# A two-layer mixer and mixture-of-experts trunk: layer 0's normalised rows from POOL to VectorE, routing by counting pairs, and a later place for layer 1's residual products

## Chip, cores and metric

One core of one Trainium2 chip. The metric is the device time of one execution in microseconds (us). The engines are named as in the profile: PE is TensorE, DVE VectorE, ACT ScalarE, POOL GpSimd, and SP the engine whose queue issues most DMAs.

## What is computed

Two layers of a trunk over 256 context rows (`ctx`) and 256 latent rows (`x`), each row 1024 wide, all in float32. Each layer mixes the rows (attention, a recurrence, latent attention, one output projection), adds the result, and then runs a mixture of 16 experts of which every row uses two. What the change touches is the end of the mixer and the choice of the experts:

```python
xl = xl + mod_l[2] * yl
hl = modulate(rms_norm(xl, norm_ffn[layer]), mod_l[3], mod_l[4])      # the normalised rows
...
scores = jax.nn.sigmoid(jnp.matmul(t, router_w))                      # 16 experts in 4 groups of 4
sel = scores + router_bias
group_score = jnp.sum(lax.top_k(sel.reshape(-1, 4, 4), 2)[0], axis=-1)
...                                                                   # the best group, in it the best 2 experts
w = jnp.take_along_axis(scores, e_idx, axis=-1); w = w / jnp.sum(w, axis=-1, keepdims=True)
y = sum over the 2 chosen experts of w * down(silu(gate(t)) * up(t))
```

Layer 0 does this for all 512 rows, layer 1 for the 256 latent rows alone.

## The kernel before

Rows are held as tiles of 128; in layer 0 there are four, t = 0 and 1 context (s = 0), t = 2 and 3 latent (s = 1). Large products are split: a weight slice is copied to a high part `wh` on ACT (line 183), the low part `wl` is the difference, made on DVE (line 184), and three products per slice go to PE (lines 164 to 166). Four `wh` and four `wl` buffers let ACT and DVE run ahead of PE by four slices.

`after_mix` is the end of the mixer. For s = 0 and then s = 1 it multiplies by the output weights in two halves of columns (`proj(s, 0)`, `proj(s, 1)`: eight weight slices and 48 products each), and its `put` adds the gated result to the rows `x[t]` (lines 918 and 919, DVE) and squares them (line 922, ACT). `flip` turns the rows for the router (line 932, PE; copied at line 934, ACT). `route(s)` adds the squares, takes the reciprocal root `rr` (lines 942 and 173 on DVE, 174 on POOL), multiplies by the router's weights (line 947, PE), copies the result (line 950, DVE), turns it (line 953, PE), sums and scales it to logits (lines 955 and 958, DVE), and calls `norm(s)` and `choose`.

`norm(s)`, in layer 0 alone, makes the normalised rows h2 = x * r * A2 + B2, which the experts read: for t < 3 the product with r on ACT (line 969), the one with A2 on POOL (line 970), for t = 3 both on DVE (line 972), and always the addition of B2 on POOL (line 973). A2 and B2 are rows that POOL's DMA queue loads (line 351) when their buffers come free: those of s = 1 after the work on the tiles of s = 0. `keep` writes the rows to DRAM (line 982, for t = 2 and 3 line 1609), from where the experts gather them.

`choose` finds for two tiles at once the best group and two experts (lines 1043 to 1094). The sums of all six pairs of a group give the group's score (lines 1048 to 1051). Then `first_max` is called three times, for the group, the first and the second expert: a maximum, two comparisons with it, another maximum, and two instructions of `put` that mark it. What comes out is `asg` (line 1082: 1 where a row uses an expert), and the two weights. `ranks` counts on PE how many rows before this one chose the same expert (lines 1105 and 1106), line 1109 makes `rm` from it on DVE, and line 978 the one-hot matrix `oh`.

`pick_early` (line 1369, PE) gathers the rows of the first fixed expert with `oh`: t = 0 and 1 before, t = 2 and 3 behind the ranks of s = 1. Its result is copied at lines 1382 (ACT) and 1383 (DVE), and the products of that expert begin. `slots` meanwhile orders the other experts by their numbers of rows; `rperm` (line 1253) names them, and SP can load their weights only when it has read it (line 1632).

In layer 1 the same `after_mix` runs for s = 1 without `norm`, and `moe1` follows: `onehot` (line 1347) and `pick` (line 1358) gather the rows of the first pair of experts, line 1461 multiplies them. The rows themselves are put into four PSUM banks by products with the identity (line 1976: four products, which the profile counts as eight). Weights flow through 20 buffers of 1 MB; SP loads the next (line 1326) when PE has finished with the buffer.

The order on each engine is set by a scheduler, which takes instructions by its own estimate of when they can run; `in_order` and `issue_after` add edges to it.

Of the kernel before, what the change touches and what calls it, by code (L numbers as in the profile page):

```python
# [73 lines left out]
class Net:  # L74
# [802 lines left out]
    def after_mix(self, l, XP, tiles, mh, ml, x, h2, ws, oh=None):  # L877
# [5 lines left out]
        with self.pool("am", side="left" if l else "right") as T:  # L883
# [52 lines left out]
            def route(s):  # L936
# [6 lines left out]
                self.rstd(ss, 2, D, rt["r"][:, i0:i0 + 2])  # L943
                a = self.at()
# [7 lines left out]
                for i in range(2):  # L952
                    nc.tensor.transpose(tp[:, i * 128:(i + 1) * 128], lt[:, i * 128:(i + 1) * 128], self.ident)
# [6 lines left out]
                if l == 0:  # L960
                    norm(s)
                self.choose(T, rt, lg, i0)

            def norm(s):
                A2, B2 = G[s][3:]
                for t in (2 * s, 2 * s + 1):
                    h, r = h2[t], rt["r"][:, t:t + 1]
                    if t < 3:
                        nc.scalar.activation(h, x[t], AF.Copy, scale=r)
                        nc.gpsimd.tensor_tensor(h, h, A2, op=OP.mult)  # L970
                    else:
                        nc.vector.scalar_tensor_tensor(h, x[t], r, A2, op0=OP.mult, op1=OP.mult)
                    nc.gpsimd.tensor_tensor(h, h, B2, op=OP.add)
# [40 lines left out]
    def routing_tiles(self, pool, l, nt):  # L1014
        r = {}
        r["r"] = pool.tile([128, nt], F32, name="rr")
        for n, w, dt in (("oh1", NE, F32), ("oh2", NE, F32), ("rk", NE, F32), ("rm", NE, F32), ("asg", NE, BF),
                         ("w1", 1, F32), ("w2", 1, F32)):
# [8 lines left out]
        r["we"] = pool.tile([128, nt, NE], F32, name="rwe")  # L1027
# [6 lines left out]
    def choose(self, T, rt, lg, i0):  # L1034
# [3 lines left out]
        t2 = slice(i0, i0 + 2)  # L1038

# [4 lines left out]
        V.scalar_tensor_tensor(sel, th, 0.5, self.rb[:, None, :].to_broadcast([128, 2, NE]), op0=OP.mult, op1=OP.add)  # L1044
# [6 lines left out]
        V.tensor_reduce(m1.rearrange("p t g -> p (t g)"), ps, axis=AX.X, op=OP.max)  # L1051
        V.tensor_scalar(sc, th, 0.5, 0.5, op0=OP.mult, op1=OP.add)

        def first_max(src, n):

            mx = T.tile([128, 2], F32, name="cmx")
            fm = T.tile([128, 2], F32, name="cfm")
            cd = T.tile([128, 2, NE], F32, name="ccd")
            V.tensor_reduce(mx, src, axis=AX.X, op=OP.max)
            for i in range(2):  # L1060
                V.scalar_tensor_tensor(cd[:, i, :n], src[:, i], mx[:, i:i + 1], self.c("adj")[:, NE - n:], op0=OP.is_ge,
                                       op1=OP.mult)
            V.tensor_reduce(fm, cd[:, :, :n], axis=AX.X, op=OP.max)
            return cd, fm

        def put(dst, cd, fm, n, op, f):

            for i in range(2):
                V.tensor_scalar(dst[:, i], cd[:, i, :n], fm[:, i:i + 1], f, op0=op, op1=OP.mult)
        g = tl("g", 4)  # L1070
        cd, fm = first_max(m1, 4)
        put(g, cd, fm, 4, OP.is_lt, -BIG)
        V.tensor_add(s4, s4, g.rearrange("p t g -> p (t g)")[:, :, None].to_broadcast([128, 8, 4]))
        o1, o2 = rt["oh1"][:, t2], rt["oh2"][:, t2]
        pen = tl("pen", NE)
        cd, fm = first_max(sel, NE)
        put(pen, cd, fm, NE, OP.is_equal, -10.0 * BIG)
        V.tensor_add(sel, sel, pen)
        put(o1, cd, fm, NE, OP.is_equal, 1.0)
        cd, fm = first_max(sel, NE)  # L1080
        put(o2, cd, fm, NE, OP.is_equal, 1.0)
        V.tensor_add(rt["asg"][:, t2], o1, o2)
        pr, w1, w2, tot = tl("pr", NE), tl("w1", 1), tl("w2", 1), tl("tot", 1)
        V.tensor_mul(pr, o1, sc)
        V.tensor_reduce(w1, pr, axis=AX.X, op=OP.add)
        V.tensor_mul(pr, o2, sc)
        V.tensor_reduce(w2, pr, axis=AX.X, op=OP.add)
        V.tensor_add(tot, w1, w2)
        V.reciprocal(tot, tot)
        V.tensor_mul(rt["w1"][:, t2], w1, tot)  # L1090
        V.tensor_mul(rt["w2"][:, t2], w2, tot)
        if "idx" not in rt:
            V.tensor_mul(rt["we"], o1, rt["w1"].to_broadcast([128, 2, NE]))
            V.tensor_mul(pr, o2, rt["w2"].to_broadcast([128, 2, NE]))
            V.tensor_add(rt["we"], rt["we"], pr)

    def ranks(self, T, rt, i0):
# [12 lines left out]
        V.tensor_copy(rt["rk"][:, t2], p3)  # L1110
# [95 lines left out]
    def slots(self, T, P, rt):  # L1206
# [59 lines left out]
        V.tensor_mul(we, rt["oh1"], rt["w1"].to_broadcast([128, nt, NE]))  # L1266
        V.tensor_mul(pr, rt["oh2"], rt["w2"].to_broadcast([128, nt, NE]))
        V.tensor_add(we, we, pr)
# [41 lines left out]
        for i, o in enumerate((rt["oh1"], rt["oh2"])):  # L1310
# [548 lines left out]
    def moe1(self, rt, x):  # L1859
# [6 lines left out]
        with ExitStack() as st:  # L1866
# [90 lines left out]
            for p in range(NE // 2):  # L1957
# [366 lines left out]
```

## Time and profile before

| | us |
|---|---|
| median of 3 runs | 1535.23 (1534.76 to 1537.57) |
| profiled execution, its own time | 1536.22 |
| its span, first to last instruction | 1534.4 |
| PE busy | 1423.4 (93%) |
| DVE busy | 928.3 (61%) |
| ACT busy | 672.4 (44%) |
| POOL busy | 110.2 (7%) |
| mean granted clock of PE | 0.977 |

How to read it: the span lacks 1.8 us of the execution's own time, which lie around it. Each engine works through its own queue in order, and waits where an operand is late. A row's idle time stands in brackets behind it, with what ended it. Two stretches matter here, the end of layer 0's mixer (about 575 to 660 us) and that of layer 1 (about 1285 to 1310 us). Behind each of them lies a long stretch of experts.

### The profile page before, as it was taken

What the parts mean: (1) busy time and instruction counts of PE and PEld (TensorE: products, weight loads), DVE (VectorE), ACT (ScalarE), POOL (GpSimd) and SP (SyncE); (2) the same over time, 40 slices, a digit from 0 to 9 for tenths busy, and PEclk for the clock granted to TensorE, in tenths of its full rate; (3) what the DMA queues carried; (4) which work ended last, traced back from release to release, by engine and by line L of the source; (5) the groups of instructions that cost most, each with busy time, mean ns of one, the idle gap of its engine ahead of it and who ended that gap; (6) DMA issues with size and microseconds to landing.
All of it is one profiled execution on the core that took longest, in us unless ns stands there. A gap on an engine that the chain in (4) does not pass through costs nothing. (4 is left out here: it accounts for less than half of the span.)

```text
span 1534.4 us, 20655 instructions
## 1 busy us (share of the span) xinstructions
PE 1423.4 (93%) x7431; PEld 931.3 (61%) x7431; DVE 928.3 (61%) x2149; ACT 672.4 (44%) x1343; POOL 110.2 (7%) x126
## 2 busy tenths in 40 slices
PE   5989999999999998789999986899999997999996
PEld 3756675587675666665545645688788775333332
DVE  4575556967554268898544748757977786423322
ACT  3343345735443235274544625555775553211112
POOL 1110000010000003200000021300001000000000
PEclk9999999999999999799999998999999999999999
DMA  7536335331125885599999994432333268999994
GB/s 314 213 138 229 138 110 199 134 112 57 56 86 204 321 304 129 196 329 366 421 420 422 420 369 164 179 110 87 121 128 100 96 226 347 362 422 424 424 423 180
DMA packets 56921, 363.63 MB, mean 237 GB/s; under 512 B 6384, under 2 KB 6384, under 8 KB 18672
## 3 DMA queue, kind: packets, MB, share of 16 engines
q1 hardware_dynamic: 47376, 328.49, 54.7%
q0 software_dynamic: 6544, 23.60, 4.7%
q10 hardware_dynamic: 2896, 10.19, 1.7%
q8 instruction: 60, 0.98, 0.3%
q14 instruction: 45, 0.37, 0.1%
HBM read 350.72 MB, written 11.54 MB: 236 GB/s over the span
## 5 line engine op out<-in xcount | busy, mean ns | idle before, releaser
L184 DVE TENSOR_TENSOR wl<-w,wh 128x512 fp32r<-128x512 f32 (+2 forms) x456 | 309.7, 696 | 183.4 <-ACT wh L183 167.2
L183 ACT CAST wh<-w 128x512 fp32r<-128x512 f32 (+2 forms) x456 | 271.0, 607 | 252.6 <-PE acc L244 126.3
L243 PE MATMUL acc<-hh,wh 128*128 128x512 f32 (+1 forms) x528 | 183.9, 348 | 0.2 <-ACT wh L183 0.2
L245 PE MATMUL acc<-hh,wl 128*128 128x512 f32 (+1 forms) x528 | 179.9, 341 | 1.4 <-DVE wl L184 1.4
L244 PE MATMUL acc<-hl,wh 128*128 128x512 f32 (+1 forms) x528 | 180.5, 342 | 0.0
L1461 PE MATMUL at<-w,xT 128*64 128x512 f32 x512 | 122.0, 600 | 1.1 <-DVE act L1466 0.8
L243 PEld LDWEIGHTS acc<-hh,wh 128*128 128x128 f32 x528 | 100.2, 190 | 31.3 <-issue 10.8
L245 PEld LDWEIGHTS acc<-hh,wl 128*128 128x128 f32 x528 | 100.3, 190 | 14.2 <-DVE wl L184 2.7
L244 PEld LDWEIGHTS acc<-hl,wh 128*128 128x128 f32 x528 | 100.2, 190 | 12.0 <-issue 2.1
L165 PE MATMUL acc<-wl,hh 128*128 128x512 f32 (+3 forms) x256 | 90.8, 355 | 8.9 <-DVE wl L184 5.4
L164 PE MATMUL acc<-wh,hh 128*128 128x512 f32 (+3 forms) x256 | 89.4, 352 | 8.5 <-ACT wh L183 3.1
L166 PE MATMUL acc<-wh,hl 128*128 128x512 f32 (+3 forms) x256 | 88.7, 349 | 0.0
L526 ACT ACTIVATE p<-at,nm 128x512 f32<-128x512 f32 (+1 forms) x96 | 59.1, 618 | 45.6 <-DVE nm L525 45.1
L1461 PE MATMUL acc<-w,xT 128*64 128x512 f32 x320 | 75.7, 599 | 1.5 <-DMA w<-in_moeu_dram 1.5
L174 POOL TENSOR_TENSOR rr<-rv,mhalf 128x1 f32<-128x1 f32 (+2 forms) x41 | 34.4, 841 | 544.0 <-DVE rv L173 538.4
L1461 PEld LDWEIGHTS at<-w,xT 128*64 128x64 f32 x512 | 33.5, 136 | 59.4 <-issue 54.9
L525 DVE TENSOR_REDUCE nm<-at 128x1 f32<-128x512 f32 (+1 forms) x96 | 56.5, 595 | 12.5 <-PE at L640 7.7
L243 PE MATMUL acc<-oh,wh 128*128 128x512 f32 (+1 forms) x160 | 59.5, 373 | 0.0
L165 PEld LDWEIGHTS acc<-wl,hh 128*128 128x128 f32 x256 | 49.1, 192 | 16.1 <-DVE wl L184 11.9
L164 PEld LDWEIGHTS acc<-wh,hh 128*128 128x128 f32 x256 | 48.8, 191 | 15.5 <-issue 4.8
L1484 PE MATMUL at<-w,aT 128*64 128x512 f32 x256 | 56.7, 595 | 0.0
L244 PE MATMUL acc<-ol,wh 128*128 128x512 f32 (+1 forms) x160 | 55.9, 350 | 0.0
(512 smaller groups left out, 2647.0 us busy)
## 6 DMA issues: line engine op xcount, KB each, us to landing
w<-in_moeg_dram SPq DMA_DIRECT2D x64, 1024.0 KB, 18.1
w<-in_moeu_dram SPq DMA_DIRECT2D x64, 1024.0 KB, 13.3
w<-in_moed_dram SPq DMA_DIRECT2D x64, 1024.0 KB, 16.8
w<-in_wmod_dram SPq DMA_DIRECT2D x48, 1024.0 KB, 6.1
w<-in_wg_dram SPq DMA_DIRECT2D x24, 1024.0 KB, 4.8
w<-in_wb_dram SPq DMA_DIRECT2D x12, 1024.0 KB, 5.0
w<-in_wout_dram SPq DMA_DIRECT2D x8, 1024.0 KB, 7.3
w<-in_wx_dram SPq DMA_DIRECT2D x4, 1024.0 KB, 8.8
```

Source lines behind the costliest of these rows:

```text
L164: nc.tensor.matmul(acc, ah, bh, start=start, stop=False)
L165: nc.tensor.matmul(acc, ah, bl, start=False, stop=False)
L166: nc.tensor.matmul(acc, al, bh, start=False, stop=stop)
L183: nc.scalar.copy(h, src)
L184: self.cut = nc.vector.tensor_sub(l, src, h.bitcast(F32))
L243: nc.tensor.matmul(a[:, :n], h[:, i, :], hh[:, k, t0:], start=k == 0, stop=False)
L244: nc.tensor.matmul(a[:, :n], h[:, i, :], hl[:, k, t0:], start=False, stop=False)
L245: nc.tensor.matmul(a[:, :n], l[:, i, :], hh[:, k, t0:], start=False, stop=k == kc - 1)
L525: nc.vector.tensor_reduce(nm, sc[h][:, :nk], axis=AX.X, op=OP.max, negate=True)
L526: nc.scalar.activation(p[:, :nk], sc[h][:, :nk], AF.Exp, bias=nm, accum_out=sm)
L1461: nc.tensor.matmul(a[i * 64:i * 64 + 64], xT[:, k], ws[i][k // 4][:, k % 4], start=k == 0, stop=k == 7, tile_position=(0, i * 64))
L1484: self.nc.tensor.matmul(ya[n][64 * j:64 * j + 64], aT[:, k, 64 * j:64 * j + 64], w[k // 2][:, k % 2, n * 512:(n + 1) * 512], start=k == 0, ...
```

## The change

In layer 0, A2 now multiplies each half of the columns as soon as `put` has it (DVE), and `norm(t)` is one DVE instruction that multiplies by r and adds B2. It is called for t = 2s right after `rr`, and for t = 2s + 1 inside `choose`, behind the call of the tanh. ACT and POOL do nothing for the rows any more. `choose` compares each expert with the three others of its group: one that wins at least two comparisons is among the two best, and a group that wins all three is chosen. One reduction adds the wins. The two experts are kept apart no longer, `we` holds both weights; layer 0 finds the first and second late in `slots`. The copy `rk` (line 1110) is gone. In layer 1 the four residual products come behind the transposition of the logits.

```diff
@@ after_mix, put
                     nc.vector.tensor_add(x[t][:, cols], x[t][:, cols], y)
+                    if l == 0:
+                        nc.vector.tensor_mul(h2[t][:, cols], x[t][:, cols], G[s][3][:, cols])
@@ after_mix, route
                 self.rstd(ss, 2, D, rt["r"][:, i0:i0 + 2])
+                if l == 0:
+                    norm(2 * s)
...
-                    nc.tensor.transpose(tp[:, i * 128:(i + 1) * 128], lt[:, i * 128:(i + 1) * 128], self.ident)
+                    self.routed = nc.tensor.transpose(tp[:, i * 128:(i + 1) * 128], lt[:, i * 128:(i + 1) * 128], self.ident)
...
-                if l == 0:
-                    norm(s)
-                self.choose(T, rt, lg, i0)
-
-            def norm(s):
-                A2, B2 = G[s][3:]
-                for t in (2 * s, 2 * s + 1):
-                    h, r = h2[t], rt["r"][:, t:t + 1]
-                    if t < 3:
-                        nc.scalar.activation(h, x[t], AF.Copy, scale=r)
-                        nc.gpsimd.tensor_tensor(h, h, A2, op=OP.mult)
-                    else:
-                        nc.vector.scalar_tensor_tensor(h, x[t], r, A2, op0=OP.mult, op1=OP.mult)
-                    nc.gpsimd.tensor_tensor(h, h, B2, op=OP.add)
+                self.choose(T, rt, lg, i0, functools.partial(norm, 2 * s + 1) if l == 0 else None)
+
+            def norm(t):
+                nc.vector.scalar_tensor_tensor(h2[t], h2[t], rt["r"][:, t:t + 1], G[t // 2][4], op0=OP.mult, op1=OP.add)
@@ choose
         nc.scalar.activation(th, lg, AF.Tanh, scale=0.5)
+        if mid:
+            mid()
...
+        def wins(src, n, name):
+            c = T.tile([128, n, 4, 3], F32, name="cc" + name)
+            w = T.tile([128, n, 4], F32, name="cw" + name)
+            for d in (1, 2, 3):
+                V.tensor_tensor(c[:, :, :4 - d, d - 1], src[:, :, :4 - d], src[:, :, d:], op=OP.is_ge)
+                V.tensor_tensor(c[:, :, d:, 3 - d], src[:, :, d:], src[:, :, :4 - d], op=OP.is_gt)
+            V.tensor_reduce(w, c, axis=AX.X, op=OP.add)
+            return w
+        we = wins(s4, 8, "e")
+        wg = wins(m1, 2, "g").rearrange("p t g -> p (t g)")
+        V.tensor_scalar(wg, wg, 2.5, None, op0=OP.is_ge)
+        asg = rt["asg"][:, t2]
+        V.scalar_tensor_tensor(asg.rearrange("p t (g e) -> p (t g) e", g=4), we, 1.5, wg[:, :, None].to_broadcast([128, 8, 4]),
+                               op0=OP.is_ge, op1=OP.mult)
         V.tensor_scalar(sc, th, 0.5, 0.5, op0=OP.mult, op1=OP.add)
-        def first_max(src, n):
...
+        pr, tot = tl("pr", NE), tl("tot", 1)
+        V.tensor_mul(pr, sc, asg)
+        V.tensor_reduce(tot, pr, axis=AX.X, op=OP.add)
         V.reciprocal(tot, tot)
...
+        V.tensor_mul(rt["we"][:, t2], pr, tot.to_broadcast(fe))
@@ slots, its last part; three instructions that made we are gone from its middle
+        V.tensor_tensor(cd, rt["asg"], self.c("adj")[:, None, :].to_broadcast(fe), op=OP.mult)
+        V.tensor_reduce(fm, cd, axis=AX.X, op=OP.max)
+        V.tensor_tensor(o1, cd, fm[:, :, None].to_broadcast(fe), op=OP.is_equal)
+        V.tensor_sub(o2, rt["asg"], o1)
+        for i, o in enumerate((o1, o2)):
...
+            V.tensor_mul(cd, rt["we"], o)
+            V.tensor_reduce(rt[f"w{i + 1}"].rearrange("p t o -> p (t o)"), cd, axis=AX.X, op=OP.add)
@@ moe1
-                    for t, xt in enumerate(x):
-                        for n in range(2):
-                            nc.tensor.matmul(res[t][n], self.ident, xt[:, n * 512:(n + 1) * 512], start=True, stop=False)
+                    with self.tc.issue_after(self.routed.ins):
...
```

On POOL, in layer 0 from the loads of s = 1 to the first gather, the queue was this (h_5002 to h_5005 are h2 of t = 0 to 3, A_5255, B_5256 and g_5251 rows of s = 1):

```order
L351 DMA g_5251<-modd_91 128x2x512
L174 TENSOR_TENSOR rr<-rv,mhalf 128x2
L970 TENSOR_TENSOR h_5002<-h_5002,A_5031 128x1024
L973 TENSOR_TENSOR h_5002<-h_5002,B_5032 128x1024
L970 TENSOR_TENSOR h_5003<-h_5003,A_5031 128x1024
L982 DMA h2d<-h_5002 128x1024
L351 DMA A_5255<-modd_92 128x2x512
L973 TENSOR_TENSOR h_5003<-h_5003,B_5032 128x1024
L351 DMA B_5256<-modd_91 128x2x512
L982 DMA h2d<-h_5003 128x1024
L174 TENSOR_TENSOR rr<-rv,mhalf 128x2
L970 TENSOR_TENSOR h_5004<-h_5004,A_5255 128x1024
```

and is now this (A_5256 and B_5257 are the rows of s = 1):

```order
L351 DMA g_5252<-modd_91 128x2x512
L351 DMA A_5256<-modd_92 128x2x512
L174 TENSOR_TENSOR rr<-rv,mhalf 128x2
L976 DMA h2d<-h_5002 128x1024
L351 DMA B_5257<-modd_91 128x2x512
L976 DMA h2d<-h_5003 128x1024
L174 TENSOR_TENSOR rr<-rv,mhalf 128x2
L1588 DMA h2d<-h_5004 128x1024
L1588 DMA h2d<-h_5005 128x1024
```

All six multiplications and additions are gone, and the load of A2 for s = 1 stands ahead of `rr`.

On DVE, in layer 0's `route(1)`, from the root's operand to the tanh's result, the rows were these:

```order
L173 TENSOR_SCALAR rv<-ss_5573 128x2
L950 COPY ytmp<-at 128x256
L972 SCALAR_TENSOR_TENSOR h_5005<-x_4998,rr,A_5255 128x1024
L955 TENSOR_REDUCE lg<-tp 128x32
L958 SCALAR_TENSOR_TENSOR lg<-lg,rr,cl 128x16 x2
L1044 SCALAR_TENSOR_TENSOR csel<-cth,rb 128x32
```

and now they are these:

```order
L173 TENSOR_SCALAR rv<-ss_5553 128x2
L184 TENSOR_TENSOR wl<-w,wh 128x512
L967 SCALAR_TENSOR_TENSOR h_5004<-h_5004,rr,B_5257 128x1024
L954 COPY ytmp<-at 128x256
L967 SCALAR_TENSOR_TENSOR h_5005<-h_5005,rr,B_5257 128x1024
L959 TENSOR_REDUCE lg<-tp 128x32
L962 SCALAR_TENSOR_TENSOR lg<-lg,rr,cl 128x16 x2
L1040 SCALAR_TENSOR_TENSOR csel<-cth,rb 128x32
```

One normalisation stands ahead of the copy of the router's products, and the other ahead of the logits' reduction.

On PE, at the end of layer 1's mixer, the residual products (L1976, into acc) stood among the router's:

```order
L947 MATMUL at<-xT,wr 32x256 x4
L1976 MATMUL acc<-x_12289,cp 128x512
L932 MATMUL tp<-cp,x_12289 128x128 x4
L1976 MATMUL acc<-x_12289,cp 128x512
L932 MATMUL tp<-cp,x_12290 128x128 x4
L1976 MATMUL acc<-x_12290,cp 128x512
L947 MATMUL at<-xT,wr 32x256 x4
L1976 MATMUL acc<-x_12290,cp 128x512
L953 MATMUL tp<-cp,ytmp 128x128 x2
L1106 LDWEIGHTS trib
```

and now stand together:

```order
L951 MATMUL at<-xT,wr 32x256 x4
L934 MATMUL tp<-cp,x_12254 128x128 x4
L934 MATMUL tp<-cp,x_12255 128x128 x4
L951 MATMUL at<-xT,wr 32x256 x4
L957 MATMUL tp<-cp,ytmp 128x128 x2
L1956 MATMUL acc<-x_12254,cp 128x512 x2
L1956 MATMUL acc<-x_12255,cp 128x512 x2
L1080 LDWEIGHTS trib
```

All four are between the transposition of the logits and the first product of the ranks.

## Rows read from the trace of the kernel before

**Rows 1.** Stretches in layer 0: PE, PEld, DVE, ACT, POOL busy us, clock, DMA share, GB/s.

```profile
575.00:585.00 10.00, 10.00 (x49) 8.19 (x48) 6.75 (x11) 6.20 (x13) 0.00 (x0) 1.00 0.50 95
...
610.30:617.30 7.00, 4.95 (x18) 3.78 (x17) 5.05 (x14) 3.67 (x9) 0.00 (x0) 0.51 0.87 286
...
645.00:650.00 5.00, 4.93 (x26) 4.90 (x27) 3.39 (x14) 0.00 (x0) 2.06 (x3) 0.50 0.01 1
```

**Rows 2.** Timeline of PE, 601 to 652 us: start, length, row, [idle before <-releaser].

```profile
602.74 0.50 PE L165 MATMUL acc<-wl,hh 128*128 128x512 f32 x1 [1.06 <-DVE wl L184]
...
609.21 0.50 PE L165 MATMUL acc<-wl,hh 128*128 128x512 f32 x1 [2.02 <-DVE wl L184]
...
613.66 0.66 PE L953 MATMUL tp<-cp,ytmp 128*128 128x128 f32 x2 [2.05 <-DVE ytmp L950]
...
630.85 0.69 PE L953 MATMUL tp<-cp,ytmp 128*128 128x128 f32 x2 [0.55 <-DVE ytmp L950]
631.33 5.13 PE L1369 MATMUL tp<-oh,h 128*128 128x128 f32 x32
...
643.96 0.17 PE L1106 MATMUL at<-rasg,trib 128*128 128x16 bf16 x1 [7.46 <-DVE rasg L1082]
...
651.77 0.48 PE L164 MATMUL acc<-wh,xh 128*128 128x512 f32 x1
```

**Rows 3.** Timeline of POOL, 596 to 639 us.

```profile
596.91 2.42 POOL L970 TENSOR_TENSOR h<-h,A 128x1024 f32<-128x1024 f32 x1 [1.26 <-ACT h L969]
...
634.17 4.64 POOL L973 TENSOR_TENSOR h<-h,B 128x1024 f32<-128x1024 f32 x2
```

**Rows 4.** Timeline of DVE, 595 to 644 us.

```profile
595.68 0.69 DVE L184 TENSOR_TENSOR wl<-w,wh 128x512 fp32r<-128x512 f32 x1 [0.84 <-ACT wh L183]
597.37 12.39 DVE L184 TENSOR_TENSOR wl<-w,wh 128x512 fp32r<-128x512 f32 x5 [1.00 <-ACT wh L183]
...
630.71 1.28 DVE L972 SCALAR_TENSOR_TENSOR h<-x,rr,A 128x1024 f32<-128x1024 f32 x1
...
632.22 4.33 DVE L958 SCALAR_TENSOR_TENSOR lg<-lg,rr,cl 128x16 f32<-128x16 f32 x2
636.85 2.02 DVE L1044 SCALAR_TENSOR_TENSOR csel<-cth,rb 128x32 f32<-128x32 f32 x1 [0.29 <-ACT cth L1043]
638.79 0.17 DVE L1052 TENSOR_SCALAR csc<-cth 128x32 f32<-128x32 f32 x1
...
639.00 0.17 DVE L1049 TENSOR_TENSOR cps<-csel 128x16 f32<-128x16 f32 x1
...
639.28 0.20 DVE L1051 TENSOR_REDUCE cm<-cps 128x8 f32<-128x48 f32 x1
639.52 0.16 DVE L1059 TENSOR_REDUCE cmx<-cm 128x2 f32<-128x8 f32 x1
```

**Rows 5.** Timeline of DVE in layer 1: the logits' scaling, with POOL idle.

```profile
1292.29 0.38 DVE L958 SCALAR_TENSOR_TENSOR lg<-lg,rr,cl 128x16 f32<-128x16 f32 x2
```

**Rows 6.** SP's longest wait from 600 to 660 us: total, times, longest.

```profile
SPq L1632 <- DVE rperm L1253: 28.8, 1, 28.8
```

**Rows 7.** Timeline of PE in layer 1, from 1290 us, and near the end.

```profile
1290.51 1.12 PE L1976 MATMUL acc<-x,cp 128*128 128x512 f32 x2
1291.47 0.38 PE L953 MATMUL tp<-cp,ytmp 128*128 128x128 f32 x2
1298.26 0.17 PE L1106 MATMUL at<-rasg,trib 128*128 128x16 bf16 x1 [6.41 <-DVE rasg L1082]
...
1300.33 5.21 PE L1358 MATMUL tp<-oh,x 128*128 128x128 f32 x32 [1.84 <-DVE oh L1347]
...
1499.43 1.08 PE L1461 MATMUL at<-w,xT 128*64 128x512 f32 x4 [0.29 <-SPq L1994]
```

**Rows 8.** Stretches in layer 1, columns as in rows 1.

```profile
1307.20:1310.00 2.80, 2.73 (x18) 0.70 (x14) 1.08 (x5) 1.53 (x2) 0.00 (x0) 1.00 0.04 12
...
1310.00:1510.00 200.00, 198.81 (x954) 74.80 (x954) 62.55 (x166) 33.97 (x66) 6.68 (x7) 1.00 1.00 417
```

More of the change, by code (lines that the diff above doesn't have):

```diff
@@ L1016, in routing_tiles @@
         r["r"] = pool.tile([128, nt], F32, name="rr")
-        for n, w, dt in (("oh1", NE, F32), ("oh2", NE, F32), ("rk", NE, F32), ("rm", NE, F32), ("asg", NE, BF),
-                         ("w1", 1, F32), ("w2", 1, F32)):
+        for n, w, dt in (("rm", NE, F32), ("asg", NE, BF), ("we", NE, F32)) + ((("w1", 1, F32), ("w2", 1, F32)) if l == 0 else ()):
             r[n] = pool.tile([128, nt, w], dt, name="r" + n)
@@ L1026, in routing_tiles @@
             r["perm"] = pool.tile([1, ND], I32, name="rperm")
-        r["we"] = pool.tile([128, nt, NE], F32, name="rwe")
         r["ls"] = pool.tile([128, 1 + 2 * XL], F32, name="rls")
@@ L1032, in routing_tiles, with choose @@
         return r
-    def choose(self, T, rt, lg, i0):
+    def choose(self, T, rt, lg, i0, mid=None):
         nc = self.nc
@@ L1038, in choose @@
         t2 = slice(i0, i0 + 2)
+        fe = [128, 2, NE]
         def tl(name, *shape):
@@ L1043, in choose @@
         nc.scalar.activation(th, lg, AF.Tanh, scale=0.5)
-        V.scalar_tensor_tensor(sel, th, 0.5, self.rb[:, None, :].to_broadcast([128, 2, NE]), op0=OP.mult, op1=OP.add)
+        if mid:
+            mid()
+        V.scalar_tensor_tensor(sel, th, 0.5, self.rb[:, None, :].to_broadcast(fe), op0=OP.mult, op1=OP.add)
         ps, m1 = T.tile([128, 8, 6], F32, name="cps"), tl("m1", 4)
@@ L1051, in choose @@
         V.tensor_reduce(m1.rearrange("p t g -> p (t g)"), ps, axis=AX.X, op=OP.max)
-        V.tensor_scalar(sc, th, 0.5, 0.5, op0=OP.mult, op1=OP.add)
-        def first_max(src, n):
[L1056 to L1088, printed above, removed]
@@ L1089, in choose @@
-        V.reciprocal(tot, tot)
[L1090 to L1095, printed above, removed]
+        def wins(src, n, name):
[6 more added lines that the diff above has]
+            return w
@@ L1109, in ranks @@
         V.scalar_tensor_tensor(rt["rm"][:, t2], p3, 1.0, rt["asg"][:, t2], op0=OP.add, op1=OP.mult)
-        V.tensor_copy(rt["rk"][:, t2], p3)
     def tokens(self, oh, out, src):
@@ L1265, in slots @@
         we, pr = rt["we"], P.tile([128, nt, NE], F32, name="spr")
-        V.tensor_mul(we, rt["oh1"], rt["w1"].to_broadcast([128, nt, NE]))
-        V.tensor_mul(pr, rt["oh2"], rt["w2"].to_broadcast([128, nt, NE]))
-        V.tensor_add(we, we, pr)
         o, tw = 0, {}
@@ L1309, in slots @@
         fr = T.tile([128, 2, nt], F32, name="xfr")
-        for i, o in enumerate((rt["oh1"], rt["oh2"])):
+        o1, o2, cd = (T.tile(fe, F32, name=n) for n in ("xo1", "xo2", "xcd"))
+        fm = T.tile([128, nt], F32, name="xfm")
+        V.tensor_tensor(cd, rt["asg"], self.c("adj")[:, None, :].to_broadcast(fe), op=OP.mult)
[3 more added lines that the diff above has]
+        for i, o in enumerate((o1, o2)):
             V.tensor_mul(ok, u, o)
             V.tensor_reduce(fr[:, i], ok, axis=AX.X, op=OP.add)
+            V.tensor_mul(cd, rt["we"], o)
+            V.tensor_reduce(rt[f"w{i + 1}"].rearrange("p t o -> p (t o)"), cd, axis=AX.X, op=OP.add)
         V.tensor_scalar(fr, fr, float(NROW), None, op0=OP.add)
@@ L1973, in moe1 @@
                     res = [[self.acc(), self.acc()] for _ in x]
-                    for t, xt in enumerate(x):
-                        for n in range(2):
-                            nc.tensor.matmul(res[t][n], self.ident, xt[:, n * 512:(n + 1) * 512], start=True, stop=False)
+                    with self.tc.issue_after(self.routed.ins):
+                        for t, xt in enumerate(x):
+                            for n in range(2):
+                                nc.tensor.matmul(res[t][n], self.ident, xt[:, n * 512:(n + 1) * 512], start=True, stop=False)
                     fetch(x[1], rt["slot"][:, 1:2])
```

## The prediction

> **What bounds the kernel now.** I read the stretches of layer 0 first, then the timelines of PE, POOL and DVE over the same 60 us side by side, then the same steps in layer 1, and last what feeds the experts. Through most of the mixer's output projection PE works without a pause, 10.00 of 10 us, while DVE has 6.75 busy [rows 1]: PE is the bound, and DVE has about a third left. That ends at 601 us. PE then waits three times for DVE, 1.06, 2.02 and 2.05 us, and once 7.46 us for `asg` [rows 2]. The reason shows where POOL and DVE are read together. While POOL multiplies and adds (its first row starts at 596.91, the last ends at 638.81) [rows 3], five DVE rows that need about 0.69 us each take 12.39 us, the scaling of the logits 4.33 us for two tiny rows, where layer 1 needs 0.38 with POOL idle, and the next row 2.02 us until 638.87, just when POOL is done [rows 4, 5]. Either engine's two-operand work on these rows seems to exclude the other's. PE's pauses also cost clock: from 610.30 to 617.30 the granted clock is 0.51, that is nearly all at 1.2 instead of 2.4 GHz, and at 645 to 650 us, behind the longest wait, it is 0.50 [rows 1].
>
> **The change, part by part.** All times of a step are places on the path to the first expert's first product, 651.77 us [rows 2].
>
> *POOL's work goes.* PE's three waits are 5.13 us. At 0.51 of the clock PE was busy 4.95 us, which is 2.5 us of work at full clock: 2.4 us. Together 7.5 us, if DVE keeps up without POOL. The two holds in `route(1)` are worth 4.33 - 0.38 = 3.95 us and 2.02 - 0.17 = 1.85 us, taking 0.17 from the next row of the same size [rows 4].
>
> *DVE gets that work.* Eight multiplications of a half cost about 0.69 us each (the row of `wl` has the same size), four rows of `norm` 1.28 each, by the row at 630.71, which goes in exchange [rows 4]: 5.5 + 5.1 - 1.3 = 9.3 us more on DVE. The four multiplications for s = 0 lie under PE's full stretch with DVE a third free: nothing. Those for s = 1 and the two norms of s = 0, 2.8 + 2.6 = 5.4 us, lie under 16 slices of `proj(1, 0)` and `proj(1, 1)`, with four slices of buffers ahead of PE: I take nothing, and 5.4 us as the other end. In `route(1)` the order puts `norm(2)` ahead of the copy of the router's products, on the path: 1.28 us lost. `norm(3)` stands where the old row of 1.28 us stood: nothing.
> The profile counts DVE as busy throughout its long rows; only the 0.69 us of the same row without POOL's work shows them as holds [rows 4]. The Trainium skill (Perfetto Trace Analysis, section Optimizing Scalar/DVE Operations) says that giving work to ScalarE or even GpSimd may make sense where VectorE is saturated, and also that the two share a read port, so that it may not help. By its first half this change goes the wrong way, and the sum would lose the 5.4 us; by its second half, and by the rows, it loses nothing. The first half is a rival below.
>
> *Loads for s = 1.* A2 is now issued ahead of `rr` on POOL's queue, since its old readers are done earlier, and B2 once the second norm of s = 0 is done. DVE's queue would stand behind either. Both are issued several us before they are read, so I take nothing; the other end is the 5.4 us again, for `wl` stands behind these reads. The writes of h2 for the gathers now wait for DVE instead of POOL and come earlier too.
>
> *Counting pairs.* From `csc` (638.79) to `asg` and the ranks (643.96) it was 5.1 us in small dependent rows [rows 2, 4]. Now 20 rows follow `csc`, most of them independent: 17 at 0.105 us apart (two steps between 638.79 and 639.00) and the last three dependent at 0.24 (639.28 to 639.52): 2.5 us, so 2.6 gained; were all 20 dependent, 0.3.
>
> *Sum to `asg`:* 7.5 - 1.3 + 3.95 + 1.85 + 2.6 = 14.6 us, at 629.3. But PE has the first half of the gather ahead of the ranks: it starts at 631.33 - 7.5 + 1.3 = 625.1 and takes 5.13 us at the low clock [rows 2], so the ranks start at 630.3: 13.6 us gained. What is late next is thus PE itself. It then has no 7.46 us pause before the second half, which ran from 645 at clock 0.50; the 4.93 us there [rows 1] would be 2.5 at full clock. I take 1.5 of these 2.5 us, since DVE's rows ahead of the copy of the result limit it. Layer 0: 15.1 us, between 12.3 (pair counting gains 0.3 alone, so that `asg` comes at 631.6, and the clock nothing) and 17.1 (2.5 us by the clock, and the first half at full clock too, so that `asg` at 629.3 decides).
> This reaches the end, for SP waits 28.8 us for `rperm` before it can load another expert [rows 6]; `rperm` follows the gather, so loads and products move together.
>
> *Layer 1.* The chain is 2.6 us shorter, and about nine small rows between `asg` and the one-hot are gone (0.9 us). But all four residual products now stand between the transposition (1291.47, perhaps 0.4 earlier) and the ranks: four at 1.0 us, since two profile rows 1.12 us long make one [rows 7]. So the ranks start at 1295.4, not at `asg`, 2.9 us earlier than 1298.26, and the gather 3.8 us earlier; at full clock its 5.21 us would be 2.6, as it ran at the lower one in the waits' wake. Low end: PE's small pauses among the router's products drop the clock, the residuals take 8.2 us and nothing is gained (+0.3). PE's gain counts only as far as the transfers move. DMA is nearly idle from 1307.2 to 1310.0 (0.04), when all buffers are full and the first comes free by PE, and then runs at 1.00 for 200 us [rows 8]; near the end PE already waits 0.29 us [rows 7], so it has no reserve there. Worth: the 2.8 us of that gap and a little more, 3.0 us (0 to 3.8).
>
> *The rest.* Seven more small DVE rows in the last part of `slots`, three fewer in its middle: beside the experts' products, nothing; without cover about 0.5 us.
>
> **Sum.** 15.1 + 3.0 = 18.1 us off the profiled execution's own 1536.2: 1518.1. That execution is 1.0 us above the median of the runs, 1535.2, so I predict 1517.
>
> **Rivals.**
> 1. *DVE becomes the bound* (the first half of the rule above): the 5.4 us, or a late A2 or B2 at the head of DVE's queue, stand before `wl`, and PE goes on waiting for it. For it: 5.05 of 7.0 us busy on DVE even from 610 on [rows 1]. Against it: four buffers. 18.1 - 5.4 = 12.7 us: 1522.5.
> 2. *Layer 1 gains nothing:* the residual products at 1.2 GHz fill the whole pause, or the stream of weights does not start earlier. For it: the 0.29 us wait at the end shows that transfers decide there [rows 7]. 15.1 us: 1520.
> 3. *Slower.* The long DVE rows come from something other than POOL (the transfers of the same microseconds, 0.87 of DMA [rows 1]). Then 7.5, 3.95 and 1.85 us stay, 5.4 + 1.3 us of work are added, the shorter chain gives 2.6: 4.1 us slower in layer 0, 1539, if layer 1 gives nothing. It decides if the rows of L184 are still above 2 us with POOL idle. The exact coincidence of the ends (638.87 and 638.81) speaks against it.
> 4. *The gain is taken back by the transfers of layer 0:* were the experts there limited by a stream that starts at a fixed time, only layer 1's 3.0 us would be left: 1532. Against it: `rperm` starts that stream [rows 6].
>
> **Chances.** My forecast 0.58; rival 1 0.16; rival 2 0.15; rival 3 0.03; rival 4 0.03; more than my sum, the clock high throughout, 0.05. A measurement of this kernel can tell about 0.2%, 3.1 us. Everything but rival 3 and a mixture of 1 and 4 is faster by more than that: 0.95 faster, 0.02 within, 0.03 slower. The forecast's ends, 12.3 + 2.3 and 17.1 + 3.8 us, are 1520.6 and 1514.3; rival 1 with the low end of the rest reaches 1524, the high clock throughout 1511. Range 1511 to 1524.
>
> **What would show it.** Right: no POOL arithmetic beyond `rr` in layer 0; no row of L184 above 0.8 us from 597 to 612; PE's waits for `wl` gone; `csel` to `asg` about 2.6 us; PE, not `asg`, deciding the ranks in both layers; the first expert about 15 us earlier; in layer 1 no hole in the transfers before the second pair. Wrong: DVE rows that stay long, PE waiting for `wl` behind `norm`, the residual products at 2 us each, or a first expert that is early with loads that aren't.

## The result, and the profile after

| | us |
|---|---|
| kernel before, median of 4 runs | 1535.59 (1534.76 to 1537.57) |
| changed kernel, median of 4 runs | 1519.29 (1517.14 to 1520.44) |
| ratio, 95% interval | 0.989 (0.9873 to 0.9908) |
| predicted | 1517 (1511 to 1524) |
| its profiled execution, and span | 1520.44, 1518.6 |

The run is 16.3 us shorter, and in a second set of runs 16.0 (1520.55 against 1536.58, 0.9899, 0.9882 to 0.9916). The sum came out, but not its parts: layer 0 gave more than predicted, and layer 1 nothing. One accident first: in this profile PE waits 1.67 us at 250 us for a load of `lw`, in a place that the change doesn't touch and that has no such wait in the second profile of the same kernel (another one below, count_only, waits 3.02 us there). So below I count from stage to stage, never from the start.

Layer 0, the timeline of PE (start, length, row, [idle before <-releaser]); it answers to [rows 2].

```profile
624.94 0.69 PE L957 MATMUL tp<-cp,ytmp 128*128 128x128 f32 x2 [2.39 <-DVE ytmp L954]
625.42 4.83 PE L1348 MATMUL tp<-oh,h 128*128 128x128 f32 x32
...
630.14 0.17 PE L1080 MATMUL at<-rasg,trib 128*128 128x16 bf16 x1
...
631.02 1.38 PE L1348 MATMUL tp<-oh,h 128*128 128x128 f32 x10 [0.56 <-DVE oh L972]
...
634.82 0.50 PE L164 MATMUL acc<-wh,xh 128*128 128x512 f32 x1
```

PE's three waits for DVE (two for `wl`, one for the copy of the router's products) and the 7.46 us for `asg` are gone. The ranks (L1080) follow the first half of the gather without a wait, and the first expert's product stands at 634.82 instead of 651.77. The view of L184 on DVE from 597 to 612 us (duration min/median/max in ns) and the timeline of POOL say why:

```profile
L184 DVE TENSOR_TENSOR wl<-w,wh x11: 679/684/693, 596.6 to 611.6; 128x512 fp32r<-128x512 f32 x11
```

```profile
598.38 1.24 POOL L174 TENSOR_TENSOR rr<-rv,mhalf 128x2 f32<-128x2 f32 x1 [1.49 <-DVE rv L173]
...
622.14 1.09 POOL L174 TENSOR_TENSOR rr<-rv,mhalf 128x2 f32<-128x2 f32 x1 [17.82 <-DVE rv L173]
```

Two small rows are all that is left of POOL's arithmetic here (seven multiplications and additions are gone, not six as written above), and none of the eleven rows is long, where five took 12.39 us [rows 4]. The stretches (columns as in rows 1) show the clock high where it was 0.51. One low stretch is left, behind the 2.39 us wait for the copy of the router's products; the same products ran at a low clock in the kernel before too (0.50 from 631 to 633 us):

```profile
610.30:617.30 7.00, 7.00 (x32) 5.77 (x31) 6.58 (x33) 3.74 (x7) 0.00 (x0) 1.00 0.68 231
...
624.00:628.00 4.00, 3.06 (x16) 3.06 (x17) 3.67 (x17) 0.23 (x1) 1.12 (x2) 0.57 1.00 415
628.00:633.00 5.00, 4.45 (x50) 4.33 (x49) 4.12 (x24) 0.00 (x0) 0.00 (x0) 1.00 0.27 107
```

That wait is `norm(2)`, as predicted, but longer than its 1.28 us, since DVE first stands 0.63 us for `rr`. The choice behind it is short (DVE):

```profile
623.26 1.28 DVE L967 SCALAR_TENSOR_TENSOR h<-h,rr,B 128x1024 f32<-128x1024 f32 x1 [0.63 <-POOL rr L174]
624.46 0.42 DVE L954 COPY ytmp<-at 128x256 f32<-128x256 f32 x1
...
627.10 0.17 DVE L1064 TENSOR_SCALAR csc<-cth 128x32 f32<-128x32 f32 x1
...
629.25 0.19 DVE L1062 SCALAR_TENSOR_TENSOR rasg<-cwe,cwg 128x32 bf16<-128x32 f32 x1
```

Layer 1, PE, first two rows of the kernel before (the router's first product and the first product of an expert), then the changed kernel; it answers to [rows 7].

```profile
1285.68 0.64 PE L947 MATMUL at<-xT,wr 128*32 128x256 f32 x8
...
1305.47 1.07 PE L1461 MATMUL at<-w,xT 128*64 128x512 f32 x2
```

```profile
1268.73 0.64 PE L951 MATMUL at<-xT,wr 128*32 128x256 f32 x8
...
1274.46 4.49 PE L1956 MATMUL acc<-x,cp 128*128 128x512 f32 x8
1278.78 0.17 PE L1080 MATMUL at<-rasg,trib 128*128 128x16 bf16 x1
...
1280.13 3.81 PE L1337 MATMUL tp<-oh,x 128*128 128x128 f32 x32 [1.12 <-DVE oh L1326]
1283.87 1.07 PE L1440 MATMUL at<-w,xT 128*64 128x512 f32 x2
...
1292.68 0.55 PE L1168 MATMUL tp<-toki,xoh 128*128 128x2 bf16 x4 [4.50 <-DVE xoh L1164]
...
1302.95 0.46 PE L1453 MATMUL tp<-cp,act 64*128 64x64 f32 x4
```

Up to the first product of an expert (L1440) it went as hoped: the residual products fill the pause, the ranks follow them without a wait, the gather takes 3.81 us instead of 5.21. From the router's first product to L1440 it takes 15.14 us instead of 19.79. Then PE waits 4.50 us for a one-hot that could have been there. DVE's row ahead of it, and POOL's issue of the write it waits for:

```profile
1292.16 0.11 DVE L1125 MEMSET yl<- 128x64 f32 x1 [6.14 <-DMA h2d<-yl]
```

```profile
1281.38 0.54 POOL L1933 DMA_DIRECT2D h2d<-yl  x1 [3.71 <-DVE yl L1931]
```

The list of overflowing rows (`extras`) takes `yl` as scratch, and the fill of that scratch stands early in DVE's order. It must wait until the write of `yl` has landed, which POOL's queue issued at 1281.38, into the full stream of weights, and the one-hots of the other pairs stand behind it. In the kernel before the wait was there already, and short:

```profile
1309.35 0.11 DVE L1152 MEMSET yl<- 128x64 f32 x1 [1.72 <-DMA h2d<-yl]
```

The stretches (columns as in rows 1):

```profile
1293.00:1296.50 3.50, 3.48 (x12) 1.08 (x14) 0.70 (x3) 0.00 (x0) 0.02 (x1) 0.50 0.25 77
...
1310.00:1500.00 190.00, 189.47 (x906) 71.75 (x904) 59.72 (x158) 32.53 (x64) 3.74 (x4) 1.00 0.98 408
```

PE's pause drops its clock to 0.50, no buffer comes free, and the transfers stand idle for most of 3.5 us: the hole of [rows 8] is there again, then the stream is nearly full (0.98).

### The profile page after: what moved, and what is told of

Its sections match the earlier page's. It is cut to its first block, busy times and chain, and to the rows that moved or that the text cites. A ratio compares the mean times of both kernels' runs of the same rounds, so it can differ in the third digit from the quotient of the medians.

```text
span 1518.6 us, 20617 instructions
## 1 busy us (share of the span) xinstructions
PE 1419.8 (93%) x7431; PEld 927.4 (61%) x7431; DVE 913.4 (60%) x2126; ACT 669.8 (44%) x1340; POOL 95.8 (6%) x119
## 5 line engine op out<-in xcount | busy, mean ns | idle before, releaser
L184 DVE TENSOR_TENSOR wl<-w,wh 128x512 fp32r<-128x512 f32 (+2 forms) x456 | 299.8, 676 | 174.7 <-ACT wh L183 158.9
L1440 PE MATMUL at<-w,xT 128*64 128x512 f32 x512 | 123.6, 607 | 0.8 <-DVE act L1445 0.8
L244 PEld LDWEIGHTS acc<-hl,wh 128*128 128x128 f32 x528 | 100.3, 190 | 11.9 <-issue 2.1
L1440 PE MATMUL acc<-w,xT 128*64 128x512 f32 x320 | 75.7, 599 | 1.4 <-DMA w<-in_moeu_dram 1.4
L1440 PEld LDWEIGHTS at<-w,xT 128*64 128x64 f32 x512 | 33.8, 138 | 59.7 <-issue 55.8
## 6 DMA issues: line engine op xcount, KB each, us to landing
w<-in_moeu_dram SPq DMA_DIRECT2D x64, 1024.0 KB, 17.1
```

What stands on the lines that cost most here:

```text
L184: self.cut = nc.vector.tensor_sub(l, src, h.bitcast(F32))
L244: nc.tensor.matmul(a[:, :n], h[:, i, :], hl[:, k, t0:], start=False, stop=False)
L1440: nc.tensor.matmul(a[i * 64:i * 64 + 64], xT[:, k], ws[i][k // 4][:, k % 4], start=k == 0, stop=k == 7, tile_position=(0, i * 64))
```

## The experiments

The table splits each profiled execution by rows of PE: A from the first transposition of layer 0's output (L932, 580.69 us in the kernel before) to the first expert's product; B from there to layer 1's first router product; C from there to the end of the span. The ratio is to the kernel before in the same set of runs. The two rows at which A starts, before and changed:

```profile
580.69 0.66 PE L932 MATMUL tp<-cp,x 128*128 128x128 f32 x4
```

```profile
582.27 0.66 PE L934 MATMUL tp<-cp,x 128*128 128x128 f32 x4
```

| kernel | A | B | C | median us | ratio to before, 95% |
|---|---|---|---|---|---|
| before | 71.08 | 633.91 | 248.72 | | |
| changed | 52.55 | 633.91 | 249.87 | 1519.29 | 0.989 (0.9873 to 0.9908) |
| again | 53.05 | 634.52 | 250.30 | 1520.55 | 0.9899 (0.9882 to 0.9916) |
| norm_only | 58.53 | 637.90 | 249.37 | 1528.84 | 0.9937 (0.9924 to 0.9951) |
| count_only | 65.25 | 632.47 | 249.53 | 1530.81 | 0.9953 (0.9936 to 0.9969) |
| res_off | 53.20 | 634.54 | 249.55 | 1519.07 | 0.9879 (0.9862 to 0.9897) |
| fix | 53.82 | 635.19 | 245.83 | 1516.68 | 0.9856 (0.9841 to 0.9871) |
| fix_res_off | 53.18 | 632.04 | 247.85 | 1517.27 | 0.9874 (0.9859 to 0.9889) |
| best | 51.41 | 633.21 | 247.35 | 1515.48 | 0.9852 (0.9833 to 0.9872) |
| pool_out | 55.42 | 636.66 | 249.15 | 1523.23 | 0.9909 (0.9889 to 0.993) |
| norm_fill | 57.79 | 637.59 | 249.39 | 1527.18 | 0.993 (0.9914 to 0.9946) |

Each of A, B and C comes from one execution. How far two of them agree is seen in the five kernels that are the same up to layer 1 (changed, again, res_off, fix, fix_res_off): A lies between 52.55 and 53.82 us there, B between 632.04 and 635.19.

### Layer 1: the fill, and the residual products

```diff
-        nc.vector.tensor_copy(cn, ct[:, :NE])
+        self.counted = nc.vector.tensor_copy(cn, ct[:, :NE])
...
-        V.memset(on, 1.0)
+        with self.tc.issue_after(self.counted.ins) if l else ExitStack():
+            V.memset(on, 1.0)
```

> The changed kernel with one thing moved: the fill of the list's scratch tile in layer 1 (DVE's MEMSET of yl) is queued behind the copy of the counts, so that it no longer stands on DVE ahead of the one-hots and waits there for the write of yl (6.14 us in the changed kernel). Theory: that wait made PE stop 4.50 us behind the one-hot, let the clock fall to 0.50 and left the transfers a hole of about 3 us (1293 to 1296.5), which ate what layer 1 had gained. Without it PE goes on at 1288, the hole shrinks or closes, and the run is 3 to 5 us shorter: 1519.3 - 4 = 1515.3 us. Rival: the write of yl is late because the stream of weights is full, and the stream decides with or without the wait; the hole moves (as it stood at 1307 to 1310 in the kernel before) and the time stays at 1519.3 +- 1.5 us.

Measured: C is 4.0 us shorter than in the changed kernel, the ratio 0.9856 (0.989 before the edit, some 5 us; the medians of the two sets are 2.6 us apart). Without the wait PE runs through, and the hole is closed (PE, and the stretches):

```profile
1288.20 1.07 PE L1441 MATMUL at<-w,xT 128*64 128x512 f32 x2
...
1293.78 7.08 PE L1441 MATMUL at<-w,xT 128*64 128x512 f32 x30
1300.80 0.46 PE L1454 MATMUL tp<-cp,act 64*128 64x64 f32 x4
...
1307.22 1.02 PE L1879 MATMUL tp<-cp,x 128*128 128x128 f32 x7 [2.38 <-DMA x<-h2d,rslot]
```

```profile
1290.00:1300.00 10.00, 10.00 (x55) 3.20 (x52) 2.58 (x8) 2.06 (x3) 2.00 (x2) 1.00 0.99 390
1300.00:1310.00 10.00, 7.03 (x38) 2.84 (x36) 2.48 (x8) 1.55 (x4) 0.94 (x1) 0.90 1.00 399
```

From the first product to the transposition of its activations (L1454) it takes 12.60 us instead of 19.08. Of these 6.5 us 2.4 are lost again: PE now waits 2.38 us for the second pair's rows, which are gathered from what that late write put in memory (in the run called best, below, the trace names the write as what POOL's gather waited for). So the theory held, with a price that neither side had named.

The residual products back in their old place:

```diff
-                    with self.tc.issue_after(self.routed.ins):
-                        for t, xt in enumerate(x):
+                    for t, xt in enumerate(x):
...
```

> The changed kernel with layer 1's residual products back where they were (among the transpositions and the router's products, not queued behind the logits). Theory A (the residual move brings little, since the shorter chain to the assignment alone lets PE reach the gather about as early, and the wait of the fill takes the rest): within 1.5 us of the changed kernel, 1519.3 us, with the ranks of layer 1 within 1 us of the changed kernel's place but the gather at 5.2 us instead of 3.8. Theory B (the prediction's 3 us for layer 1 hang on the residual products): 1522.3 us.

> Both of the two edits before: the fill queued behind the counts, and the residual products back among the router's products. Theory A of the run before: within 1.5 us of the kernel with the fill alone, so about 1515 to 1517 us. Theory B (once the fill is out of the way the residual move shows its worth): 3 us more than the fill alone, about 1518.5 us. If the fill is worth nothing (its rival), both are at 1519 to 1522 us.

Measured: C is 249.55 without the fix, 0.3 us from the changed kernel, and 247.85 with it, 2.0 us longer than with the fix alone (245.83). Theory A holds for the first. For the second the two measures disagree: the medians are 0.6 us apart, within theory A's 1.5, and C speaks for something nearer to B. So a worth of the residual move is not shown; the fill's edit is worth 1.7 us of C here. The traces show where the 2.0 us of C lie. With the products in their old place and the fix, PE's clock is 0.51 from 1275.75 to 1280.75 us, the gather takes 6.45 us, and the transfers lose part of a stretch. Late in layer 1 PE is even 0.84 us ahead of the kernel with the fix alone (188.53 against 189.37 us behind the start of C, L1454 at 1454.28 and 1462.44), and then it waits for the last weights, as the other doesn't (stretch, columns as in rows 1, then PE, of fix_res_off):

```profile
1285.75:1290.75 5.00, 5.00 (x32) 1.47 (x28) 1.53 (x5) 1.03 (x1) 0.40 (x1) 1.00 0.66 220
```

```profile
1478.63 1.93 PE L1441 MATMUL at<-w,xT 128*64 128x512 f32 x6 [1.75 <-SPq L1974]
```

That is the prediction's own rule at work: PE's gain counts only as far as the transfers move.

### Layer 0: the parts alone

> The kernel before with the normalised rows on DVE by halves alone: the old choice by first maxima stays (shared signature, the second norm still behind the tanh), and so does the place of layer 1's residual products. Theory: nearly all of layer 0's gain is POOL's work gone. From csel to asg it stays 5.1 us instead of 2.45, so that asg comes 1.9 us behind the first half of the gather and decides the ranks; layer 1 is as before. 1535.6 - 18.5 + 1.9 + about 1 = 1520 us (by the prediction's own terms, 7.5 - 1.3 + 3.95 + 1.85 and 1.5 by the clock: 1522). No row of L184 above 0.8 us between 597 and 612. Rival: the rows on DVE are no better than on POOL and the shorter choice carries the gain: 1527 us or more, with PE's waits for wl still there.

> The kernel before with the choice by counting pairs alone (and the weights of the two experts worked out later, as in the changed kernel): POOL keeps the normalised rows, layer 1's residual products stay. Theory: POOL holds DVE until 638.8 us, so the shorter choice can give only its own 2.6 us in layer 0; PE has still stood for some 5 us before the ranks, so the second half of the gather runs at the low clock, 4.9 us. In layer 1 the chain is 2.6 us shorter, but the fill's wait for the write of yl (as in the changed kernel) takes most of it. 1537.4 - 2.6 - (0 to 2) = 1533 to 1535 us, so that the two parts alone (9 and 3 us) give less than the 18 us of both together. Rival (the parts add up: counting is worth as much alone as it is on top of the norm, some 9 us): 1528 us.

Both expectations were missed in the run's time. The norm alone gives 8.5 us between the medians (9.7 by the ratio), not 16; counting alone 6.4 (7.2 by the ratio), not 3. The time of the norm alone is that of its rival, but the rival's sign is absent: PE's waits for `wl` are gone, A is 12.55 us shorter, and B is 4.0 us longer. In A the parts do add up: 12.55 and 5.83 us, together 18.4, and 17.88 in the kernel that has both with layer 1's products in their old place (res_off). Where counting's 5.8 us are, PE shows (norm_only, then count_only):

```profile
632.16 0.17 PE L1102 MATMUL at<-rasg,trib 128*128 128x16 bf16 x1 [4.70 <-DVE rasg L1078]
...
639.33 0.50 PE L164 MATMUL acc<-wh,xh 128*128 128x512 f32 x1
```

```profile
635.97 0.69 PE L953 MATMUL tp<-cp,ytmp 128*128 128x128 f32 x2 [1.54 <-DVE ytmp L950]
...
644.86 0.17 PE L1086 MATMUL at<-rasg,trib 128*128 128x16 bf16 x1 [3.35 <-DVE rasg L1068]
...
651.40 0.49 PE L164 MATMUL acc<-wh,xh 128*128 128x512 f32 x1
```

POOL's last sum ends 58.12 us behind the start of A in the kernel before and 56.35 in count_only, and from there to the ranks it is 5.15 [rows 2, 3] and 2.36 us. The latter, 2.8 us, is the short chain itself. The former, 1.8 us, was not expected. Part of it is the *first* half's choice (s = 0), whose rows stood in DVE's queue among those of the projection, and whose tail stood ahead of the second half's `rv`, on which POOL's rows wait (DVE before, then count_only):

```profile
626.63 0.69 DVE L919 TENSOR_TENSOR x<-x,ytmp 128x512 f32<-128x512 f32 x1
...
629.31 0.16 DVE L173 TENSOR_SCALAR rv<-ss 128x2 f32<-128x2 f32 x1
```

```profile
630.73 1.28 DVE L919 TENSOR_TENSOR x<-x,ytmp 128x512 f32<-128x512 f32 x2
...
633.28 0.17 DVE L173 TENSOR_SCALAR rv<-ss 128x2 f32<-128x2 f32 x1
```

From the end of the last addition to `rv` it is 1.99 and 1.27 us, which shows 0.7 of the 1.8 us. Of the rest 0.8 us lie ahead of that addition, and what they hang on was not split; 0.3 are POOL's own product (L970, 2.65 and 2.35 us). And 1.3 us more lie behind the ranks (6.54 to the first product instead of 7.81). On top of the norm (norm_only, then res_off), counting takes the ranks from 9.25 to 5.88 us behind the transposition of the logits and the rest from 7.17 to 4.68.

Is that last part the clock? The norm-only kernel with 28 idle transpositions in the 4.70 us:

```diff
+                idle = self.at()
+                with self.tc.issue_after(self.half.ins):
+                    for k in range(28):
+                        nc.tensor.transpose(idle[:, k % 4 * 128:(k % 4 + 1) * 128], self.ident, self.ident)
                 self.ranks(T, rt, 2)
...
+                self.half = last
```

> The kernel with the norm on DVE alone and the old choice, with 28 idle transpositions of the identity on PE (into a bank that nobody reads, about 3.7 us at full clock) between the first half of the gather and the ranks, where that kernel's PE waits 4.70 us for asg. Theory: the shorter choice gave 6 us in layer 0 where its own chain is 2.5 us shorter, because PE no longer stands and so the second half of the gather runs at full clock (4.68 us from the ranks to the first product instead of 7.17). With the idle work in the wait and the same asg, ranks to first product take 4.7 to 5.2 us and the run is about 2 us shorter: 1528.8 - 2.2 = 1526.5 us. Rival (the second half is long for another reason, DVE's rows before it): 7.2 us again, 1528.8 us or more.

(`self.half` is the last product of the gather's first half.) Measured: 6.41 us instead of 7.17, between the expectation and its rival, and a time that can't be told from the kernel without them. The stretches (columns as in rows 1) of the kernel without them, then of this run:

```profile
632.00:635.00 3.00, 2.16 (x18) 2.00 (x18) 2.77 (x15) 0.00 (x0) 0.00 (x0) 0.50 0.01 3
```

```profile
633.00:635.00 2.00, 1.39 (x15) 1.38 (x15) 1.85 (x12) 0.00 (x0) 0.00 (x0) 1.00 0.01 4
635.00:637.00 2.00, 2.00 (x13) 2.00 (x11) 2.00 (x9) 0.00 (x0) 0.54 (x2) 0.54 0.00 0
```

The low clock came later, not away: PE still stood 1.43 us for `asg` and 0.68 for the one-hot. That the second half is slow because the clock is at its lower level is shown: its first ten products take 2.47 us in the kernel before, at 0.50 [rows 1], and 1.38 in the changed one, at 1.00. That filling the pause cures it is not shown.

### POOL and DVE

```diff
                     if t < 3:
                         nc.scalar.activation(h, x[t], AF.Copy, scale=r)
-                        nc.gpsimd.tensor_tensor(h, h, A2, op=OP.mult)
...
-                    nc.gpsimd.tensor_tensor(h, h, B2, op=OP.add)
```

> The kernel before without POOL's arithmetic on the normalised rows: the products with A2 (three tiles) and the sums with B2 (four tiles) are left out, so the experts of layer 0 read rows without them; ScalarE's scaling, every load, write, choice and order stay. Nothing is added on DVE. Theory: POOL's work alone makes DVE's rows long. The five long rows of L184 become 0.69 us each, PE's three waits for wl (5.13 us) and the two holds in the choice (3.95 and 1.85 us) go, and from the first transposition of layer 0 to the first expert's product it takes about 58 us instead of 71.1, as in the kernel with the norm on DVE (58.5), although that one has 9.3 us more work on DVE: so those 9.3 us cost nothing. Total 1525 to 1529 us. Rival 3 of the prediction (the long rows come from the transfers): L184 rows still above 2 us with POOL idle, 1535 us.

In the next one both lines become `nc.gpsimd.tensor_scalar` with a constant, 2.0 and 1.0:

> The kernel before with POOL's seven operations on the normalised rows of one operand instead of two: the products with A2 become products with a constant, the sums with B2 sums with a constant (the experts of layer 0 read rows without A2 and B2). Theory A, what the prediction wrote (two-operand work on either engine shuts the other's out): POOL's one-operand rows leave DVE alone, L184 rows are 0.69 us and the time is that of the kernel with POOL's arithmetic left out, within 2 us, unless POOL itself becomes late. Theory B (any POOL arithmetic on SBUF holds DVE's two-operand rows): L184 rows of 2.4 us on average as before, PE's waits for wl there, 1533 to 1537 us.

L184 on DVE from 595 to 612 us: before, without POOL's arithmetic, and with one operand (ns min/median/max), then POOL's row beside it in the last:

```profile
L184 DVE TENSOR_TENSOR wl<-w,wh x6: 677/2690/3756, 595.7 to 609.1; 128x512 fp32r<-128x512 f32 x6
```

```profile
L184 DVE TENSOR_TENSOR wl<-w,wh x11: 681/684/693, 595.4 to 611.1; 128x512 fp32r<-128x512 f32 x11
```

```profile
L184 DVE TENSOR_TENSOR wl<-w,wh x11: 675/692/1370, 594.9 to 611.2; 128x512 fp32r<-128x512 f32 x11
```

```profile
599.03 3.06 POOL L973 TENSOR_SCALAR h<-h 128x1024 f32<-128x1024 f32 x1
```

POOL's work makes the rows long, so rival 3 is out; and it is above all its *two-operand* work: POOL's rows with one operand last as long (2.78 to 3.06 us), and DVE's rows of L184 keep a median of 692 ns beside them, 1370 at most. They are not quite free: small rows of the choice are still held, this one for 0.97 us where it takes 0.18 without POOL's arithmetic (DVE, one operand):

```profile
628.42 0.97 DVE L1078 TENSOR_TENSOR csel<-csel,cpen 128x32 f32<-128x32 f32 x1
```

The ranks come 2.6 us later than in pool_out, and A, all that counts of that kernel, is 58.34 us, 2.9 longer, more than the 2 us of theory A (1603.47 us in all, since its layer 1 chooses otherwise and the loop over overflowing rows runs). The Trainium skill (GPSIMD Engine Reference, section 1. Specifications) names contention with DVE instructions that have two SBUF inputs; the traces agree (L184 has two: a median of 2690 ns beside POOL's arithmetic, 684 without it), and add that POOL's own count of operands matters too.

A is 55.42 us without POOL's arithmetic, 3.1 less than with the same work on DVE (58.53). So DVE's additional 9.3 us cost 3.1 us, 2.4 of them up to the ranks; the expectation that they cost nothing was wrong.

### A version that is faster than both

The fix, and `norm(2 * s)` behind the copy of the router's products instead of ahead of it:

```diff
-                if l == 0:
-                    norm(2 * s)
                 a = self.at()
...
                 nc.vector.tensor_copy(lt, a[:, :256])
+                if l == 0:
+                    norm(2 * s)
```

> The changed kernel with two things moved: the fill of the list's scratch tile behind the counts (as in the run called fix) and, in layer 0, the normalisation of the third tile behind the copy of the router's products instead of ahead of it. Theory: the fill gives 4 us in layer 1; the copy comes 1.3 us earlier, PE no longer waits 2.39 us for it and so keeps its clock for the first half of the gather (4.1 us instead of 4.83), and then asg, which stands behind the same DVE work as before, decides the ranks: 0.5 to 1.5 us in layer 0. 1519.3 - 4 - 1 = 1514.3 us (1513 to 1516.5). Rival: the gain of the fill is taken back by the stream of weights, and the norm only trades one wait for another: 1517.5 us or more.

> The changed kernel once more, unaltered, beside the next one on the same chip: 1519 us (1517 to 1522). From the first transposition of layer 0's last tiles to the first expert's product 52 to 54 us, in layer 1 from the first product of the first expert pair to the transposition of its activations 17 to 19 us, with the wait of the fill for the write of yl there again. If that wait was an accident of one execution: 12.6 us there and some 1516 us.

Measured side by side: 1515.48 and 1520.55 us, 5.1 us. The wait of the fill was there again in the unaltered kernel, with the same 4.50 us on PE. C is 247.35 us, 2.5 to 3 us shorter than in the changed kernel, though 1.5 longer than in the first run of the fix: here the four residual products take 5.93 us (4.58 there), and PE waits 0.95 us for the last weights. In layer 0 the new order is worth 1.1 to 1.6 us of A, and `asg` now decides the ranks, by 0.61 us. The clock was not kept as expected: the first half of the gather takes 4.61 us, not 4.1 (PE):

```profile
622.82 0.69 PE L957 MATMUL tp<-cp,ytmp 128*128 128x128 f32 x2 [0.53 <-DVE ytmp L952]
623.30 4.61 PE L1349 MATMUL tp<-oh,h 128*128 128x128 f32 x32
...
628.56 0.17 PE L1080 MATMUL at<-rasg,trib 128*128 128x16 bf16 x1 [0.61 <-DVE rasg L1062]
```

## Why the prediction came out, step by step

- **POOL's work goes, 12.0 us with the cost of `norm(2)`:** right in sum, 11.9 us up to the ranks and 12.55 of A with the norm alone. Both sides of it were too small: POOL's arithmetic left out gives 15.7 us (14.3 up to the ranks; predicted 13.3), DVE's additional work takes 3.1 (2.4 up to the ranks; predicted 1.3, with 6.7 as the far end: the 5.4 beside it).
- **Counting pairs, 2.6 us:** the chain itself was right, 2.34 us from `csc` to the end of `asg` where 2.5 was predicted. As a part of layer 0 it was mis-sized: 5.8 us alone, 5.3 on top of the norm. Missing were the 1.8 us by which POOL's last sum ends earlier (of which the first half's choice ahead of `rv` is shown for 0.7) and what lies behind the ranks (1.3).
- **PE's first gather half decides the ranks:** right (630.14, no wait).
- **The second half by the clock, 1.5 us:** too small, ranks to first product went from 7.81 to 4.68 us. DVE's rows ahead of the copy, for which I held back, are no limit: the clock is 1.00 and PE waits 0.56 us. Layer 0 gave 18.5 (again: 18.0) instead of 15.1 us, above the upper end of 17.1.
- **Layer 1, 3.0 us:** this is the step that failed. The gather came 3.25 us earlier (predicted 3.8) and the first product behind it 4.65, but C is 1.2 us longer, not 3.0 shorter. "PE's gain counts only as far as the transfers move" was the right question; I took them to follow the gather, and missed DVE's fill of `yl`, whose wait was in the kernel before too, 1.72 us long. Without it layer 1 gives 2.9 us in the profile of fix and 1.4 in that of best. The forecast's lower end also took 2.3 us for layer 1, for which it named no row, though its own range for it began at 0.
- **The rest and the transfers of layer 0:** B is the same to 0.1 us in the two profiles, 0.6 us longer in the second one of the changed kernel. Rival 4 may have some truth where layer 0 is shortened and the old choice stays: B is 4.0 us longer in norm_only, 3.7 in norm_fill and 2.8 in pool_out, against a spread of 3.2 us among the five kernels above. In norm_only PE waits 3.63 us for the first rows gathered from `h2d` (1.26 before, none in the changed kernel). Why that gather lands later there was not tried.
- **Rivals:** 2 is the one that came true for layer 1, by another mechanism than the two it named; 1 is refuted by the missing waits for `wl`, though DVE's work did cost 3.1 us, and 3 by pool_out. The forecast's time held by luck: layer 0's 3.4 us more and layer 1's 4.2 us less than predicted nearly cancel; in the profiled execution the 1.67 us for `lw` come on top.

## What to carry to other kernels

When a stage comes earlier, look for instructions that stand early in an engine's order only because they depend on nothing but a buffer: a fill of a borrowed scratch tile inherits the wait for whatever transfer last read that tile, and holds all behind it. Cost a shorter chain in every place where it runs, also where it only stands ahead of something else in a queue, and with the clock of what follows. Judge an engine that is "busy" beside another by the same row without the neighbour.

## What was not expected of the hardware

DVE's long two-operand rows go on at nearly full speed beside POOL's one-operand rows, which last as long as POOL's two-operand ones (L184: median 692, at most 1370 ns, against 2690). The two writes of 512 KB from POOL's queue landed 11.6 and 10.7 us after their issue in the changed kernel, where the DMA share was 0.99 (1277 to 1292.2 us); in the kernel before the second took 7.7 us, with a share of 0.71 while it ran. That is what makes a wait for such a write expensive.
